# Layer 0's attention in an encoder kernel: the rotary key's products, the conv taps and the modulation pacing are placed anew

## Chip, cores and metric

One core of a Trainium2 chip runs the whole program in one launch. The metric is device time in microseconds (us), the median of several runs; less is better.

## What is computed

Two layers of an encoder on 256 tokens of width 2048, all in float32. Each layer has two halves:

```
mod = silu(c) @ w_mod[l] + b_mod[l]          # six vectors of 2048: shift, scale, gate for each half
h = layer_norm(x) * (1 + scale_m) + shift_m
proj = h @ w_in[l]                            # split into four head groups A, B, C, D
y = concat(gmlp(A), attention(B), short_conv(C), conformer_conv(D)) @ w_out[l]
x = layer_norm(ALPHA * x + (1 + gate_m) * y, post_mix_g, post_mix_b)
h = layer_norm(x) * (1 + scale_f) + shift_f
x = layer_norm(ALPHA * x + (1 + gate_f) * conv_ffn(h), post_ffn_g, post_ffn_b)
```

Group B is latent attention: query and key/value latents are RMS-normed and expanded by `mla_w_uq` and `mla_w_ukv`, a rotary part is added to queries and keys, a masked softmax follows in blocks of 128 queries. Group D's conv has 31 taps along the tokens. `w_mod[l]` alone has 2048 x 12288 numbers, so the six vectors of each layer are a large part of the bytes that the kernel reads.

## The kernel before

Weights are streamed from memory in units of up to 1 MB and multiplied on TensorE (PE) in the order of the program. Layer 0's mixers run through `by_blocks` (L1297) with plain float32 products; most of the rest splits each weight into a high part (`whi`, made on ScalarE, ACT) and a low part (`wlo`, made on VectorE, DVE) and makes three products. Within each engine instructions go in program order; a scheduler fixes that order when the kernel is built. SyncE (SP) issues the loads, also in order.

**Where the attention sits.** After the B group (the latents), the C group (`C_c` products, eight units of 16 products 128 x 256) keeps PE busy while the attention's steps go in between. `mix_b` (L1001) normalises the latents and starts `attend` (L1054), a generator; at each `yield` it puts itself into the list of postponed steps, and one unit of C's products is placed before it goes on. In its first stretch the latents are turned by PE (`ps_q`, `ps_kv`), ACT writes the queries' latents `qg`, DVE writes the rotary key's parts `kc` and the key/value latents `kvr`; PE makes the rotary key `ps_kr` out of `kc`, ACT copies it into `rope`; then follow `ps_qn`, `ps_qr`, `ps_kn`, `ps_v`. A pool of two PSUM buffers serves all of these. Three yields stand between the first two softmaxes and the transposes of their results (`ps_pT`).

**The conv taps.** Group D's 31 taps (`taps`, L859) are queued in a background list and run a few at a time with the units: for a tap ACT makes four activations into a `scaled` buffer (four such buffers) and DVE adds them in one instruction to `convD` (L871). `attended` (L1091) names the instruction behind which ACT's scaled activations are put.

**The modulation stream.** `w_mod`'s blocks of 1 MB are fetched and used in a fixed order: 16 steps for GATE_M (`macc`, L203 and L205), 16 for SHIFT_F, 16 for SCALE_F (L194, each writes a column of sums; the last is followed by the small addition L285 which makes the vector `mod`), then GATE_F, and layer 1's. How many are issued is decided by a credit: `phase` (L311) sets a rate, `pump` (L314) adds it once for each unit loaded and issues one block for each whole credit. `more_mods` (L801) adds the rate `attend` once, and is called four times in `attend`; `mix_b` issues three blocks (MODS_AHEAD) beyond the credit. In layer 0 the units are 8 of B, 8 of C, 8 of `out` (out projection, columns 0 to 1023), 4 of `out_next`, and four of `out_last` with rate 0. What is still missing is forced by `need` (L320), which `out_proj` calls through `before()` after the products of its first token tile: SHIFT_F and SCALE_F must be complete for the norm that follows.

**The end of the out projection.** For each token tile t: `yg`, `x` and the statistics on DVE (L632 to L636), the norm's aggregation (L567), two passes over x (L673, L676), sums of squares on ACT (`junk`, L688), then `xn` (ACT), transposes `ps_xT` (PE, L586), `hN` (scale and shift of the feed-forward's input by `mod`, L118), and the products `first` of the feed-forward (PE, L534).

Of the kernel before, what the change touches and what calls it, by code (L numbers as in the profile page):

```python
# [15 lines left out]
S = 256  # L16
# [16 lines left out]


RATES = [
    dict(B=1.3, attend=1.3, C=1.9, out=1.0, out_next=1.55, out_last=0.0, up=0.7, down=0.7, down_next=0.7, down_last=0.0),
    dict(D=1.0, U=0.0, V=0.0, B=0.0, C=0.0, E=0.9, attend=0.0, out=0.6, out_next=0.6, out_last=0.0, up=0.3, down=0.7, down_next=0.7, down_last=0.0),
]

# [47 lines left out]
def encoder_kernel(ctx: ExitStack, tc: tile.TileContext, A: dict, consts: bass.AP, out: bass.AP):  # L87
# [24 lines left out]
        return accp.tile([P, 512], F32, tag="acc", name=name)  # L112

    def mm(o, lhsT, rhs, start, stop):
        pe.matmul(o, lhsT, rhs, start=start, stop=stop, skip_group_check=True)  # L115

    def ident_act(o, i, scale, bias):
        return act.activation(out=o, in_=i, func=AF.Identity, scale=scale, bias=bias)  # L118
# [1 line left out]
    def slot(name, dtype=F32):  # L120
        return slotp.tile([P, 1024], dtype, tag="slot", name=name)
# [205 lines left out]

    pending = []
    postponed = []
    background = []  # L330

    def flush():
# [79 lines left out]
    def group(w, c0, width, name, then, ntm=0, nk=2, hF=None, bg=0, spare=0):  # L412
# [6 lines left out]
        def products(item, u):  # L419
            if u == 0:  # L420
                box["c"] = [acc_tile(f"{name}_c{i}") for i in range((ncm + 1) // 2)]
                box["t"] = [[acc_tile(f"{name}_t{t}{i}") for i in range(ntm)] for t in range(2)]
                box["h"] = list(hT)
            for part in (range(0, min(4, ncm)), range(4, ncm)):
                for k, (hi, lo) in enumerate(item):
                    kt = u * nk + k
                    st, sp = kt == 0, kt == KT - 1
                    for i in part:
                        o = box["c"][i // 2][:, (i % 2) * S : (i % 2 + 1) * S]
                        off = slice(i * P, (i + 1) * P)  # L430
                        first = st and i % 2 == 0
                        if lo is None:
                            mm(o, hi[:, off], hF(kt), first, sp)
                        else:
                            xh, xl = (h[:, kt % 2, :] for h in box["h"][kt // 2][:2])
                            mm(o, hi[:, off], xh, first, False)
                            mm(o, hi[:, off], xl, False, False)
                            mm(o, lo[:, off], xh, False, sp)
            for k, (hi, lo) in enumerate(item):
                kt = u * nk + k  # L440
                st, sp = kt == 0, kt == KT - 1
                for i in range(ntm):
# [347 lines left out]
    def mixers(l, w_in, Y, hF=None, first_mod=None, quarter=None):  # L790
# [7 lines left out]
        CLB = lambda j: pm[:, 149 + j : 150 + j]  # L798
        attended, stepped = [], []

        def more_mods():  # L801
# [40 lines left out]
        def conv_d(glu):  # L842
# [16 lines left out]
            def taps(k):  # L859
# [7 lines left out]
                for j in range(4):  # L867
                    i = act.activation(out=t[:, j, :n], in_=glu[:, j, :n], func=AF.Copy, scale=CW(k, j))
                    if attended:
                        tc.add_manual_dep(i.ins, attended[0], order_dep, reason="the latents come first")  # L870
                dve.tensor_tensor(out=yd[:, :, 30 - k :], in0=yd[:, :, 30 - k :], in1=t[:, :, :n], op=ALU.add)  # L871

            if hF is not None:
                for k in range(30, -1, -1):
# [126 lines left out]
        def mix_b(wide, narrow):  # L1001
# [14 lines left out]
            if hF is not None:  # L1016
                for _ in range(MODS_AHEAD):
                    next(mods, None)
                stepped.append(last_step[0])

            lat = [tmp_tile("lat0"), tmp_tile("lat1")]
            q01 = tmp_tile("lat2").rearrange("p (t c) -> p t c", t=2)
# [31 lines left out]
        def attend(WQ, WKV, lat, q01, rr):  # L1054
            qg = slot("qg")[:, :768].rearrange("p (j s) -> p j s", j=3)
            kvr = slot("kvr")[:, :768].rearrange("p (j s) -> p j s", j=3)

            def behind(i):
                if stepped:
                    tc.add_manual_dep(i.ins, stepped[0], order_dep, reason="these steps' weights land before the latents turn")  # L1060

            def turn(ps, o, parts):
                for t in range(2):
                    n = parts[t].shape[1]
# [6 lines left out]
                act.activation(out=qg[:, j, :], in_=by, func=AF.Copy, scale=QG(j))  # L1071
            ps = ms_tile("ps_q")
            by = turn(ps, 0, [lat[t][:, 320:448] for t in range(2)])
            act.activation(out=qg[:, 2, :], in_=by, func=AF.Copy, scale=QG(2))
            by = turn(ps, S, [lat[t][:, 256:320] for t in range(2)])
            kc = tmp_tile("kc")
            behind(dve.tensor_tensor(out=kc[0:64, 0:S], in0=by[0:64, :], in1=cosT[0:64, :], op=ALU.mult))
# [4 lines left out]
                behind(dve.tensor_scalar(out=kvr[:, j, :], in0=by, scalar1=KVG(j), scalar2=None, op0=ALU.mult))  # L1082

            rope = slot("rope").rearrange("p (j s) -> p j s", j=4)
            ps = ms_tile("ps_kr")
            mm(ps[:, :S], idup, kc[0:64, 0:S], True, False)
            mm(ps[:, :S], rotdup, kc[0:64, S : 2 * S], False, True)
            pool.memset(rope[64:128, 2, :], 0.0)
            pool.memset(rope[0:64, 3, :], 0.0)
            act.copy(rope[0:64, 2, :], ps[0:64, :S])  # L1090
            attended.append(act.copy(rope[64:128, 3, :], ps[64:128, :S]).ins.name)  # L1091
            more_mods()

            qn = slot("qn").rearrange("p (j s) -> p j s", j=4)
# [99 lines left out]

            p0 = softmax(0, 0)
            p1 = softmax(1, 0)
            yield
            yield
            yield
            turned(p0, 0, 0)  # L1200
# [478 lines left out]
```

## Time and profile before

| | |
|---|---|
| runs | 2221.61, 2224.57, 2225.37 us; median 2224.57 |
| profiled execution | 2224.01 us, of which 2222.2 us are the span in the trace (1.8 us lie around it) |
| mean granted TensorE clock | 0.996 |
| PE busy | 2195.2 us, 99% of the span |
| DVE busy | 1715.7 us, 77% |
| ACT busy | 1092.7 us, 49% |
| bytes moved | 603.96 MB, mean 272 GB/s |

A row of the timeline gives the start, the busy time, engine, line, operation, output and inputs, tile shape and count; in brackets the idle time ahead of it and what ended it. A row of the windows gives a stretch in us, its length, and for each engine the busy time and number of instructions, then the granted TensorE clock (PEclk, 1.00 is full speed), and the share and rate of the DMA engines.

### The profile page before, as it was taken

How to read it: one execution, taken by the hardware profiler on the slowest of the kernel's cores; microseconds unless marked ns; L12 is line 12 of the kernel's file. 1: busy time of each engine (PE TensorE's matmuls, PEld its weight loads, DVE VectorE, ACT ScalarE, POOL GpSimd, SP SyncE). 2: the span in 40 equal slices, each digit the busy share in tenths (PEclk: the TensorE clock that was granted, in tenths of full speed). 3: DMA queues.
4: the chain of work that ended last, by engine and by line, in shares of the span. 5: the costliest groups of instructions: out<-in, count | busy, mean ns of one | idle time of the engine just before them, and what ended most of it. 6: DMA issues, size and time to landing. Idle time of an engine off the chain costs nothing. (4 is left out here: it accounts for less than half of the span.)

```text
span 2222.2 us, 28375 instructions
## 1 busy us (share of the span) xinstructions
PE 2195.2 (99%) x10880; PEld 1803.2 (81%) x10880; DVE 1715.7 (77%) x2197; ACT 1092.7 (49%) x1677; POOL 23.2 (1%) x38
## 2 busy tenths in 40 slices
PE   9999999999999999999999999999999999999997
PEld 6776875588888888888868978868888888888886
DVE  5657996799898989989958988867776656575776
ACT  3132731655554445545655545465455545454552
POOL 0000000000000000000000000000000000000000
PEclk9999999999999999999999999999999999999999
DMA  9999889688988888888758547847765555555553
GB/s 392 417 374 390 336 329 391 222 331 312 339 316 319 327 324 320 316 332 325 281 189 313 175 149 263 323 177 260 262 212 189 180 199 190 190 189 191 191 198 140
DMA packets 94034, 603.96 MB, mean 272 GB/s; under 512 B 10565, under 2 KB 10693, under 8 KB 29125
## 3 DMA queue, kind: packets, MB, share of 16 engines
q1 hardware_dynamic: 93898, 602.15, 73.7%
q8 instruction: 85, 1.39, 0.3%
q14 instruction: 51, 0.42, 0.1%
HBM read 600.01 MB, written 2.10 MB: 271 GB/s over the span
## 5 line engine op out<-in xcount | busy, mean ns | idle before, releaser
L390 ACT CAST whi<-wraw 128x1024 fp32r<-128x1024 f32 (+1 forms) x608 | 634.5, 1047 | 672.9 <-PE g_c L115 202.3
L391 DVE TENSOR_TENSOR wlo<-wraw,whi 128x1024 fp32r<-128x1024 f32 (+1 forms) x608 | 730.4, 1212 | 288.4 <-ACT whi L390 281.6
L115 PE MATMUL v_c<-hT,whi 128*128 128x512 f32 x1408 | 489.6, 391 | 0.0
L115 PE MATMUL g_c<-hT,whi 128*128 128x512 f32 x1280 | 444.7, 391 | 0.0
L115 PE MATMUL v_c<-hT,wlo 128*128 128x256 f32 x1408 | 394.4, 280 | 0.0
L115 PE MATMUL d<-whi,a 128*128 128x512 f32 x1344 | 386.1, 389 | 0.0
L115 PE MATMUL g_c<-hT,wlo 128*128 128x256 f32 x1280 | 358.4, 280 | 0.0
L194 DVE SCALAR_TENSOR_TENSOR wmod<-wmod,crep 128x2048 f32<-128x2048 f32 x128 | 292.0, 2285 | 38.3 <-DMA wmod<-in_w_mod_dram 37.5
L115 PEld LDWEIGHTS v_c<-hT,whi 128*128 128x128 f32 x1408 | 263.3, 187 | 57.6
L115 PEld LDWEIGHTS d<-whi,a 128*128 128x128 f32 x1344 | 252.2, 188 | 52.2
L115 PEld LDWEIGHTS g_c<-hT,whi 128*128 128x128 f32 x1280 | 239.4, 187 | 52.5
L115 PEld LDWEIGHTS v_c<-hT,wlo 128*128 128x128 f32 x1408 | 266.1, 189 | 0.2
L115 PEld LDWEIGHTS g_c<-hT,wlo 128*128 128x128 f32 x1280 | 241.9, 189 | 0.1
L115 PE MATMUL d<-wlo,a 128*128 128x512 f32 x672 | 232.9, 389 | 0.0
L205 DVE SCALAR_TENSOR_TENSOR macc<-wmod,cact,macc 128x2048 f32<-128x2048 f32 x60 | 140.7, 2346 | 19.5 <-DMA wmod<-in_w_mod_dram 19.1
L115 PEld LDWEIGHTS d<-wlo,a 128*128 128x128 f32 x672 | 126.2, 188 | 26.3
L115 PE MATMUL o<-whi,a 128*128 128x512 f32 x320 | 90.5, 390 | 0.0
L410 DVE TENSOR_TENSOR a<-g,a 128x512 fp32r<-128x512 f32 x132 | 88.6, 683 | 0.0
L534 PE MATMUL first<-wexact,hN 128*128 128x512 f32 x192 | 85.5, 595 | 1.2 <-ACT hN L118 0.8
L409 ACT CAST a<-g 128x512 fp32r<-128x512 f32 x132 | 81.1, 615 | 8.3 <-PE d L115 4.8
L1440 DVE SCALAR_TENSOR_TENSOR u<-g,par,u 128x254 f32<-128x254 f32 (+1 forms) x176 | 74.2, 476 | 0.3 <-ACT u L118 0.2
L115 PEld LDWEIGHTS o<-whi,a 128*128 128x128 f32 x320 | 59.9, 188 | 12.7 <-ACT whi L390 0.4
(317 smaller groups left out, 2384.4 us busy)
## 6 DMA issues: line engine op xcount, KB each, us to landing
wmod<-in_w_mod_dram SPq DMA_DIRECT2D x192, 1024.0 KB, 6.8
wraw<-in_ffn_w_up_dram SPq DMA_DIRECT2D x168, 1024.0 KB, 5.4
wraw<-in_ffn_w_down_dram SPq DMA_DIRECT2D x88, 1024.0 KB, 4.9
wexact<-in_w_in_dram SPq DMA_DIRECT2D x64, 512.0 KB, 10.0
wraw<-in_w_in_dram SPq DMA_DIRECT2D x24, 1024.0 KB, 5.2
wraw<-in_w_out_dram SPq DMA_DIRECT2D x22, 1024.0 KB, 5.5
wexact<-in_w_out_dram SPq DMA_DIRECT2D x20, 512.0 KB, 12.4
wexact<-in_ffn_w_up_dram SPq DMA_DIRECT2D x16, 512.0 KB, 6.2
```

The costliest lines, as they stand in the source:

```text
L115: pe.matmul(o, lhsT, rhs, start=start, stop=stop, skip_group_check=True)
L194: i = dve.scalar_tensor_tensor(out=raw, in0=raw, scalar=1.0, in1=crep, op0=ALU.mult, op1=ALU.mult, accum_out=col)
L205: i = dve.scalar_tensor_tensor(out=acc, in0=w, scalar=col, in1=acc, op0=ALU.mult, op1=ALU.add)
L390: held(act.copy(hi[:, :m], r), "cast")
L391: i = dve.tensor_tensor(out=lo[:, :m], in0=r, in1=hi[:, :m].bitcast(F32), op=ALU.subtract)
L409: act.copy(hi, src)
L410: dve.tensor_tensor(out=lo, in0=src, in1=hi.bitcast(F32), op=ALU.subtract)
L534: i = pe.matmul(ps, hN[kt // 4][:, kt % 4, t * P : (t + 1) * P], parts[kt], start=kt == 0, stop=kt == KT - 1, skip_group_check=True,)
L1440: dve.scalar_tensor_tensor(out=u[:, sh:], in0=x[:, : S - sh], scalar=col(k, j), in1=u[:, sh:], op0=ALU.mult, op1=ALU.add)
```

## The change

Five edits, all in layer 0's attention or beside it (line numbers in the rows below: those of the changed kernel are a few higher).

1. The rate of C goes from 1.9 to 2.17, and `mix_b` takes one such rate off the credit.
2. The rotary key's products `ps_kr`, its copies and the first `more_mods` come behind a new `yield`; its first product is ordered behind the last product of a unit of C. (`mm` returns its instruction for that.)
3. One of the three yields behind the first softmaxes goes.
4. The wide tap additions on DVE are ordered behind the third modulation step of `mix_b`, as `kc` and `kvr` are already.
5. `attended` names the activation that writes `qg`'s third part, and no longer the last `rope` copy.

```diff
-    dict(B=1.3, attend=1.3, C=1.9, out=1.0, out_next=1.55, out_last=0.0, ...),
+    dict(B=1.3, attend=1.3, C=2.17, out=1.0, out_next=1.55, out_last=0.0, ...),
...
     def mm(o, lhsT, rhs, start, stop):
-        pe.matmul(o, lhsT, rhs, start=start, stop=stop, skip_group_check=True)
+        return pe.matmul(o, lhsT, rhs, start=start, stop=stop, skip_group_check=True)
...
                         if lo is None:
-                            mm(o, hi[:, off], hF(kt), first, sp)
+                            last_product[0] = mm(o, hi[:, off], hF(kt), first, sp).ins.name
...
-                dve.tensor_tensor(out=yd[:, :, 30 - k :], in0=yd[:, :, 30 - k :], in1=t[:, :, :n], op=ALU.add)
+                behind(dve.tensor_tensor(out=yd[:, :, 30 - k :], in0=yd[:, :, 30 - k :], in1=t[:, :, :n], op=ALU.add))
...
                 for _ in range(MODS_AHEAD):
                     next(mods, None)
                 stepped.append(last_step[0])
+                pace["credit"] -= RATES[l]["C"]
...
-            act.activation(out=qg[:, 2, :], in_=by, func=AF.Copy, scale=QG(2))
+            i = act.activation(out=qg[:, 2, :], in_=by, func=AF.Copy, scale=QG(2))
+            attended.append(i.ins.name)
...
             rope = slot("rope").rearrange("p (j s) -> p j s", j=4)
+            yield
             ps = ms_tile("ps_kr")
-            mm(ps[:, :S], idup, kc[0:64, 0:S], True, False)
+            i = mm(ps[:, :S], idup, kc[0:64, 0:S], True, False)
+            if hF is not None:
+                tc.add_manual_dep(i.ins, last_product[0], order_dep, reason="a unit's products cover the latents' steps")
             mm(ps[:, :S], rotdup, kc[0:64, S : 2 * S], False, True)
...
-            attended.append(act.copy(rope[64:128, 3, :], ps[64:128, :S]).ins.name)
+            act.copy(rope[64:128, 3, :], ps[64:128, :S])
             more_mods()
...
             p0 = softmax(0, 0)
             p1 = softmax(1, 0)
-            yield
             yield
             yield
             turned(p0, 0, 0)
```

How the order moves, at the two places where most of it does. First, PE at the attention's start, before (`ps_kv` are the turned key/value latents, `ps_kr` the rotary key, `C_c` the conv group's accumulators):

```order
L1065 MATMUL ps_kv<-cst,lat_1061 128x128 [waits Activation_49]
L1065 MATMUL ps_kv<-cst,lat_1062 128x128
L115 MATMUL ps_kr<-kc,cst 128x256 [waits DVE_49,PE_49]
L1065 MATMUL ps_kv<-cst,lat_1061 128x128 [waits DVE_49]
L1065 MATMUL ps_kv<-cst,lat_1062 128x128
L115 MATMUL ps_kr<-kc,cst 128x256
L115 MATMUL ps_qn<-qg,wq_1042 128x256 [waits DMAHW4_49,DVE_49]
```

and after the change, at the same place on PE:

```order
L1067 MATMUL ps_kv<-cst,lat_1061 128x128 [waits Activation_49]
L1067 MATMUL ps_kv<-cst,lat_1062 128x128
L115 MATMUL C_c_1094<-hF_115,wexact 128x256 [waits DMAHW4_49]
L115 MATMUL C_c_1094<-hF_115,wexact 128x256
L1067 MATMUL ps_kv<-cst,lat_1061 128x128 [waits DVE_49]
L1067 MATMUL ps_kv<-cst,lat_1062 128x128
L115 MATMUL C_c_1095<-hF_115,wexact 128x256 x2
L115 MATMUL C_c_1094<-hF_115,wexact 128x256 [waits DMAHW5_49]
```

Two products of a C unit stand between the two pairs of `ps_kv`, the other 14 behind them, and the two of `ps_kr` behind those. On ACT, the rotary key's copies (L1096, L1097) stand after the change behind the scaled activations of taps 248 to 240 wide, 33 of them behind the last `qg`; this is the end of that row:

```order
L873 ACTIVATE scaled<-gluD,par 128x241 [waits DVE_49]
L873 ACTIVATE scaled<-gluD,par 128x241 [waits Activation_49] x3
L873 ACTIVATE scaled<-gluD,par 128x240 [waits DVE_49]
L873 ACTIVATE scaled<-gluD,par 128x240 [waits Activation_49]
L1096 COPY rope<-ps_kr 64x256 [waits PE_49]
L1097 COPY rope<-ps_kr 64x256
L873 ACTIVATE scaled<-gluD,par 128x240 [waits Activation_49] x2
```

Before, both copies came directly behind the last `qg`, ahead of all scaled activations.

Second, the end of the out projection. On SP after the change, the loads from the norm's gains (`gb`) on; `wmod_2110` is the last block of SCALE_F:

```order
L643 DMA gb_2064<-in_post_mix_g_dram 128x2048
L643 DMA gb_2066<-in_post_mix_b_dram 128x2048
L375 DMA wexact_2078<-in_ffn_w_up_dram 128x1024
L375 DMA wexact_2080<-in_ffn_w_up_dram 128x1024
L375 DMA wexact_2082<-in_ffn_w_up_dram 128x1024
L375 DMA wexact_2084<-in_ffn_w_up_dram 128x1024
L375 DMA wexact_2086<-in_ffn_w_up_dram 128x1024
L375 DMA wexact_2088<-in_ffn_w_up_dram 128x1024
L375 DMA wexact_2090<-in_ffn_w_up_dram 128x1024
L375 DMA wexact_2092<-in_ffn_w_up_dram 128x1024
L193 DMA wmod_2110<-in_w_mod_dram 128x2048
L295 DMA wmod_2363<-in_w_mod_dram 128x2048
```

Before, that block stood 18 loads of the out projection, gains and feed-forward earlier, right behind the block ahead of it. On DVE before, its step (`wmod_2022`) and the vector's addition (`mod_0_4`) stood here, with the out projection's columns 1024 to 1535:

```order
L636 BN_STATS st_o00_1601<-x0_91 128x6
L632 TENSOR_TENSOR yg_2061<-o0_102410_1969,gate_0_2_1216 128x512
L194 SCALAR_TENSOR_TENSOR wmod_2022,sums_0_4_1597<-wmod_2022,crep_101 128x2048
L633 SCALAR_TENSOR_TENSOR x1_92<-x1_92,yg_2061 128x512
L285 TENSOR_TENSOR mod_0_4_2025<-sums_0_4_1597,par_93 128x16
L636 BN_STATS st_o01_1602<-x1_92 128x6
```

After the change they stand on DVE with the second token tile's last columns, behind the whole norm of the first tile:

```order
L710 SCALAR_TENSOR_TENSOR rs_o0r0_2159<-sums_o00_2141,rs_o0r0_2159 128x1
L633 TENSOR_TENSOR yg_2228<-o0_153610_2047,gate_0_2_1236 128x512
L634 SCALAR_TENSOR_TENSOR x1_92<-x1_92,yg_2228 128x512
L637 BN_STATS st_o01_1602<-x1_92 128x6
L194 SCALAR_TENSOR_TENSOR wmod_2110,sums_0_4_1597<-wmod_2110,crep_101 128x2048
L568 BN_AGGR mv_o0p1_2232<-st_o01_1602 128x2
L285 TENSOR_TENSOR mod_0_4_2113<-sums_0_4_1597,par_93 128x16
```

The step has moved past about twenty instructions of the first tile's norm, and the first tile's `hN` on ACT now names DVE among what it waits for, as it did not before. On PE after the change, `first` is split:

```order
L587 MATMUL ps_xT<-cst,xn 128x128 [waits Activation_49]
L587 MATMUL ps_xT<-cst,xn 128x128 x3
L535 MATMUL first_2211<-wexact,hN_2163 128x512 [waits DMAHW1_49,Activation_49]
L587 MATMUL ps_xT<-cst,xn 128x128 [waits Activation_49]
L587 MATMUL ps_xT<-cst,xn 128x128 x3
L587 MATMUL ps_xT<-cst,xn 128x128 [waits Activation_49]
L587 MATMUL ps_xT<-cst,xn 128x128 x3
L535 MATMUL first_2211<-wexact,hN_2163 128x512
```

Before, four products `first` of `hN_2163` stood ahead of the third and fourth group of `ps_xT`; now one does.

More of the change, by code (lines that the diff above doesn't have):

```diff
@@ L35 @@
 RATES = [
-    dict(B=1.3, attend=1.3, C=1.9, out=1.0, out_next=1.55, out_last=0.0, up=0.7, down=0.7, down_next=0.7, down_last=0.0),
+    dict(B=1.3, attend=1.3, C=2.17, out=1.0, out_next=1.55, out_last=0.0, up=0.7, down=0.7, down_next=0.7, down_last=0.0),
     dict(D=1.0, U=0.0, V=0.0, B=0.0, C=0.0, E=0.9, attend=0.0, out=0.6, out_next=0.6, out_last=0.0, up=0.3, down=0.7, down_next=0.7, down_last=0.0),
@@ L329, in encoder_kernel @@
     postponed = []
+    last_product = [None]
     background = []
@@ L799, in mixers, with behind @@
         attended, stepped = [], []
+        def behind(i):
+            if stepped:
+                tc.add_manual_dep(i.ins, stepped[0], order_dep, reason="these steps' weights land before the latents turn")
         def more_mods():
@@ L1056, in attend @@
             kvr = slot("kvr")[:, :768].rearrange("p (j s) -> p j s", j=3)
-            def behind(i):
-                if stepped:
-                    tc.add_manual_dep(i.ins, stepped[0], order_dep, reason="these steps' weights land before the latents turn")
             def turn(ps, o, parts):
```

## The prediction

> **What bounds the kernel now.** First the page: busy times, then the chain that ended last.
>
> ```profile
> span 2222.2 us, 28375 instructions
> PE 2195.2 (99%) x10880; PEld 1803.2 (81%) x10880; DVE 1715.7 (77%) x2197; ACT 1092.7 (49%) x1677; POOL 23.2 (1%) x38
> ...
> PE 33%; DVE 1%; ACT 0%; issue 0%; DVEq 0%; POOL 0%; ACTq 0%
> ```
>
> PE is busy for all but 2222.2 - 2195.2 = 27.0 us, so a change that removes no product can gain only from idle time and from time at a lowered clock. So I read the timeline of PE where the change works, from 200 us on.
>
> ```profile
> 202.77 0.33 PE L1065 MATMUL ps_q<-cst,lat 128*128 128x128 f32 x1 [0.96 <-ACT lat L1035]
> 202.93 7.07 PE L115 MATMUL C_c<-hF,wexact 128*128 128x256 f32 x32
> ...
> 210.68 0.77 PE L1065 MATMUL ps_q<-cst,lat 128*128 128x128 f32 x4 [0.35 <-ACT qg L1071]
> 211.68 0.44 PE L1065 MATMUL ps_kv<-cst,lat 128*128 128x128 f32 x2 [0.23 <-ACT qg L1071]
> 213.57 1.19 PE L115 MATMUL ps_kr<-kc,cst 64*128 64x256 f32 x2 [1.45 <-DVE kc L1078]
> ...
> 216.52 7.14 PE L115 MATMUL ps_qn<-qg,wq 128*128 128x256 f32 x24
> ```
>
> One unit of C is 16 products, shown as 32 records in 7.07 us: 0.44 us a product. The rotary key waits 1.45 us for `kc`. `ps_qn`, 24 records, takes 7.14 us where 24/32 of 7.07 would be 5.3: a second loss. The windows show it; I cut them where the clock changes, every 3.41 us.
>
> ```profile
> 199.51:202.92 3.41, 2.45 (x9) 1.00 1.04 426
> 209.75:213.16 3.41, 1.79 (x11) 1.00 1.00 414
> 213.16:216.58 3.42, 3.01 (x7) 0.50 1.02 410
> 216.58:219.99 3.41, 3.41 (x8) 0.50 1.02 405
> 219.99:223.40 3.41, 3.41 (x17) 1.00 1.05 430
> 1281.54:1284.95 3.41, 1.44 (x10) 1.00 0.00 0
> 1284.95:1288.36 3.41, 3.23 (x11) 0.50 0.00 0
> 1288.36:1291.78 3.42, 3.42 (x18) 1.00 0.87 307
> ```
>
> The number behind the counts is the granted clock. A window with 1.62 us idle (3.41 - 1.79) was followed by one at 0.50; one with 0.96 idle (3.41 - 2.45) was not. At 0.50, a window with 0.41 idle was followed by a second at 0.50; windows with 0.18 and 0 idle were followed by full speed. I use this as the rule of the case: from between 0.96 and 1.62 us idle the next window runs at half speed, and between 0.18 and 0.41 us of idle within it bring another.
>
> **The attention, what goes.** The 1.45 us wait; and half of the 3.01 + 3.41 = 6.42 us of work done at half speed, 3.2 us. Together 4.7 us, 0.21% of the span: the most that the intended part can give.
>
> **The attention, what comes.** DVE first:
>
> ```profile
> 205.44 7.33 DVE L205 SCALAR_TENSOR_TENSOR macc<-wmod,cact,macc 128x2048 f32<-128x2048 f32 x3 [8.16 <-DMA wmod<-in_w_mod_dram]
> 212.68 0.41 DVE L1077 TENSOR_TENSOR kc<-ps_q,cst 64x256 f32<-64x256 f32 x1
> ...
> 213.34 0.47 DVE L1082 TENSOR_SCALAR kvr<-ps_kv,par 128x256 f32<-128x256 f32 x1
> ```
>
> `kc` and the first `kvr` stand behind three modulation steps, and stay there. The first `kvr` ends at 213.81. In the changed order, the second pair of `ps_kv` waits for it, with only two products of C ahead: 211.9 + 0.9 = 212.8, so 1.0 us idle, about 0.4 of it ahead of 213.16. That window then has 0.35 + 0.23 + 0.4 = 1.0 us idle, near the 0.96 that cost nothing: I take no drop. Then 14 products (6.2 us) end near 220.2, `ps_kr` near 221.1, the first half of `ps_qn` near 223.7. The tap additions, now behind the third step, stand behind that first `kvr` too and delay none of this. Now ACT:
>
> ```profile
> 216.56 0.36 ACT L1090 COPY rope<-ps_kr 64x256 f32<-64x256 f32 x1 [4.93 <-PE ps_kr L115]
> ...
> 217.33 2.85 ACT L868 ACTIVATE scaled<-gluD,par 128x248 f32<-128x248 f32 x7
> ...
> 224.41 7.49 ACT L868 ACTIVATE scaled<-gluD,par 128x245 f32<-128x245 f32 x19
> ```
>
> A scaled activation takes 2.85/7 = 0.41 to 7.49/19 = 0.39 us. With `attended` moved, 33 of them stand ahead of the two `rope` copies: from the last `qg`, near 211.6, 33 x 0.40 = 13.1 us, so the copies run from 224.7 to 225.5. The second half of `ps_qn` needs the PSUM buffer that they read, from 223.7: PE waits 1.8 us, all of it inside the window 223.40 to 226.82. That is above 1.62, so I take one window at half speed, a loss of 1.7. Sum: -4.7 + 1.0 + 1.8 + 1.7 = **-0.2**. Ends: -1.9 without the drop, +1.5 with a second half-speed window.
>
> The yield that goes brings the transposes `ps_pT` one unit (7.07 us) nearer to the softmax. Bounds: nothing, or the rest of the chain of DVE and ACT; two units, 14.1 us, still cover it, and I take nothing.
>
> By the Trainium skill (TensorE: Matmul & The Clock Gate, Part 1: The HAM clock gate) the clock halves only after an idle window of about 3.4 us, and the window runs freely. The rows above differ on the first: 1.62 us idle in a window was enough here. By the page's rule the attention's 1.8 us wait would cost no clock, and the attention would give -1.9. On the second they agree: all the cuts fit one grid of 3.41 us.
>
> **The pacing.** Before, layer 0's credit up to the last units: 8 x 1.3 + 8 x 1.9 + 4 x 1.3 + 8 x 1.0 + 4 x 1.55 = 45.0, and 45 + 3 blocks ahead = 48 = 16 each of GATE_M, SHIFT_F and SCALE_F: just enough. After: 8 x 2.17 - 2.17 = 15.19 takes the place of 15.2, the sum is 44.99, and 47 blocks are paced. The last block of SCALE_F is left for `need`, behind eight loads of `w_out`, two of `gb` and eight of `ffn_w_up`.
>
> The two rows are SP's timeline, which issues the loads:
>
> ```profile
> 374.83 18.63 SPq L374 DMA_DIRECT2D wexact<-in_ffn_w_up_dram  x8
> 393.56 1.22 SPq L295 DMA_DIRECT2D wmod<-in_w_mod_dram  x2
> ```
>
> The second view is the windows, with PE, PEld, DVE, ACT and POOL ahead of the clock:
>
> ```profile
> 404.00:405.00 1.00, 1.00 (x4) 0.50 (x3) 0.93 (x2) 1.00 (x4) 0.00 (x0) 1.00 0.30 123
> ```
>
> In that place two other blocks were issued from 393.56 and the DMA engines fall quiet in the window from 404 (share 0.30, 123 GB/s); the first of the two must have landed near 402. Its step is then placed on DVE:
>
> ```profile
> 375.86 2.28 DVE L194 SCALAR_TENSOR_TENSOR wmod<-wmod,crep 128x2048 f32<-128x2048 f32 x1
> ...
> 403.97 0.69 DVE L636 BATCH_NORM_STATS2 st_o<-x 128x6 f32<-128x512 f32 x1
> 404.70 0.26 DVE L567 BATCH_NORM_AGGREGATE mv_o0p<-st_o 128x2 f32<-128x24 f32 x1
> ```
>
> Before, the step ran from 375.86, 27 us ahead of its use. After, the step stands between the two rows at 404: from 404.6, 2.28 us, the aggregation, then the addition: `mod` near 407.3. Who waits for it:
>
> ```profile
> 402.45 2.90 ACT L118 ACTIVATE hN<-ps_xT,mod,mod 128x128 f32<-128x128 f32 x8 [0.95 <-PE ps_xT L586]
> ```
>
> `hN` started at 402.45; now not before 407.35, and its eight run to 410.3. On PE:
>
> ```profile
> 401.81 1.04 PE L586 MATMUL ps_xT<-cst,xn 128*128 128x128 f32 x8
> 402.96 3.70 PE L534 MATMUL first<-wexact,hN 128*128 128x512 f32 x8
> 406.50 1.04 PE L586 MATMUL ps_xT<-cst,xn 128*128 128x128 f32 x8
> 407.38 10.46 PE L534 MATMUL first<-wexact,hN 128*128 128x512 f32 x24
> 417.68 1.04 PE L586 MATMUL ps_xT<-cst,xn 128*128 128x128 f32 x8
> ```
>
> PE stands from 402.85 to 407.8 (5.0 us against 0.1), makes one `first` (0.43 us), and the fourth group of `ps_xT` needs the PSUM buffer that the second four `hN` read until 410.3. From about 410.4 there remain four transposes (0.45) and 31 `first` at 10.30/24 = 0.43 (13.3 us): the second tile's `ps_xT` start at 424.1 and not 417.68: **+6.4**. The second tile's norm is 2.3 us later on DVE and does not become the bound, since PE is 6.4 later. This idle fills the window 404.31 to 407.72 (the same grid) wholly, so the clock falls at 407.72. Within that half-speed window PE still idles about 0.7 us between `first` and the two groups of transposes, more than 0.41, so by the case's rule the next one is slow too: 0.4 for the first (its other work is waiting anyway) and 1.7 for the second. **+8.5** in all; bounds +6.4 and +8.5.
>
> **Behind it.** The late block also takes one of four `raw` buffers:
>
> ```profile
> 426.31 1.28 DVE L203 TENSOR_SCALAR macc<-wmod,cact 128x2048 f32<-128x2048 f32 x1
> ```
>
> The second `wraw` of the next stage is issued when this step has given its buffer back; after the change one more step (2.4 us, the row of three: 7.33/3) must run first. Bounds 0 and 2; the steps' blocks now have 6 us more to land and run, so I take 0. The remaining program keeps its order but for a shift of one step, and I take nothing for it.
>
> **Sum.** Against the profiled execution: 2224.0 - 0.2 + 8.5 = **2232.3**. That execution lies 0.56 below the median of the runs, 2224.57.
>
> **Rivals.** A measurement of this kernel can tell about 0.2%, 4.4 us: 2220.1 to 2229.0 count as no change.
> - *The change works as meant* and the late block is hidden: 2224.0 - 4.7 = 2219.3, faster. It needs `mod` ready by 402.45, that is its step done on DVE ahead of the second tile's `yg` and not behind it; the order speaks against it, and so does the load, which lands near 402. Chance 0.05.
> - *The attention pays in full*, because ACT runs the scaled activations later or `ps_qn` does not wait for the copies, and the late block costs as above: 2224.0 - 4.7 + 8.5 = 2227.8, no change. ACT is in order and the 33 stand first, which speaks against. Chance 0.15.
> - *The clock holds* in the attention and falls for one window only at the late block: 2224.0 - 1.9 + 6.4 + 0.4 = 2228.9, on the edge of no change. For it: in layer 1, 1.97 us idle cost one window, not two. Chance 0.2, split evenly between no change and slower. By the Trainium skill's rule on the clock (the page named above) it would come out so, since only the wait near 408 fills a whole window.
> - *Everything drops*: a second slow window in the attention and the full 2 us for `wraw`: 2224.0 + 1.5 + 8.5 + 2 = 2236.0. Chance 0.1.
>
> My forecast has the remaining 0.5 (2229.5 to 2234). Faster 0.05; no change 0.15 + 0.10 = 0.25; slower 0.70. The range reaches from just below the second rival to just below the last, 2226.5 to 2235.5.
>
> **What would show it.** Right: on PE an idle row of some 5 us ahead of `first` near 408, released by ACT `hN`; on DVE the L194 step behind the last statistics; in the attention no wait for `kc`, a wait of about 1 us at the second `ps_kv` and one near 1.8 us inside `ps_qn`, released by ACT; a clock of 0.50 behind the wait at 408. Wrong: `hN` near 402 with no wait for DVE; a full clock throughout; or a new wait of PE in the stage behind 425 us.

## The result, and the profile after

| | before | after |
|---|---|---|
| runs on one chip, median of 5 | 2223.16 us (2221.61 to 2225.37) | 2232.47 us (2229.25 to 2234.63) |
| profiled execution | 2224.01 us, span 2222.2 | 2233.07 us, span 2230.9 |
| mean granted TensorE clock | 0.996 | 0.996 |

The ratio is 1.0037, with a 95% interval of 1.0027 to 1.0048: slower by 6 to 10.7 us, as forecast (2232.3). How much of that agreement is luck is what the rest is about. First the page of after, busy times by engine:

```profile
span 2230.9 us, 28359 instructions
PE 2197.3 (98%) x10880; PEld 1801.5 (81%) x10880; DVE 1715.6 (77%) x2197; ACT 1092.8 (49%) x1677; POOL 25.4 (1%) x38
```

The span is 8.7 us longer; PE's busy time grew by 2.1 and its idle time from 27.0 to 33.6. To place the 8.7 us I compare when PE reaches the same instruction in both traces. The attention's start lies 0.5 us earlier in after already (its first `C_c` at 202.41 against 202.93), ahead of the first edit, so 0.5 is taken off each difference below.

**The attention.** PE's timeline of after; the bracket is the idle time ahead of the row and what ended it:

```profile
213.04 0.44 PE L1067 MATMUL ps_kv<-cst,lat 128*128 128x128 f32 x2 [0.47 <-DVE kvr L1085]
213.31 6.21 PE L115 MATMUL C_c<-hF,wexact 128*128 128x256 f32 x28
...
220.51 2.86 PE L115 MATMUL ps_qn<-qg,wq 128*128 128x256 f32 x12
224.72 2.86 PE L115 MATMUL ps_qn<-qg,wq 128*128 128x256 f32 x12 [1.36 <-ACT rope L1097]
```

ACT's timeline of after, the scaled activations and the last copy that the second `ps_qn` waits for:

```profile
211.10 12.94 ACT L873 ACTIVATE scaled<-gluD,par 128x248 f32<-128x248 f32 x33
...
224.31 0.37 ACT L1097 COPY rope<-ps_kr 64x256 f32<-64x256 f32 x1
```

The windows of after at that wait, PE alone: length, busy time and count, granted clock, share and rate of the DMA engines:

```profile
221.64:225.06 3.42, 2.06 (x11) 1.00 0.98 404
225.06:228.47 3.41, 3.21 (x15) 1.00 0.34 67
```

Both foretold waits are there, behind `kvr` (0.47) and behind the 33 activations and the copies (1.36), but the clock stayed at full speed: each half of `ps_qn` takes 2.86 us, where all 24 records took 7.14 in before, with half clock up to 219.99. The next mark is `ps_mean`, behind C's last product: 292.72 against 295.50, so the attention and C gain 2.78 - 0.52 = **2.26 us**.

**Given back.** The out projection follows. PE's timeline of before:

```profile
295.50 1.89 PE L115 MATMUL ps_mean<-convD,ones 128*128 128x256 f32 x8
...
313.47 0.73 PE L115 MATMUL o<-wlo,a 128*128 128x512 f32 x2
...
319.50 0.59 PE L115 MATMUL ps_rD<-dgD,ones 128*128 128x256 f32 x2
```

and of after:

```profile
292.72 1.89 PE L115 MATMUL ps_mean<-convD,ones 128*128 128x256 f32 x8
294.92 14.00 PE L115 MATMUL o<-wexact,ya 128*128 128x512 f32 x32 [0.31 <-DMA wexact<-in_w_out_dram]
...
312.64 0.73 PE L115 MATMUL o<-wlo,a 128*128 128x512 f32 x2 [1.47 <-DVE wlo L392]
...
318.69 0.59 PE L115 MATMUL ps_rD<-dgD,ones 128*128 128x256 f32 x2
```

At `ps_rD` the lead is down from 2.78 to 0.81 us: **1.97 given back**, 0.31 to a load of `w_out` and 1.47 to the first low part `wlo`, which DVE makes. DVE's timeline of before between C's end and that `wlo`, the first and the last of four steps (two more of the kind start at 299.46 and 305.58):

```profile
296.38 2.28 DVE L194 SCALAR_TENSOR_TENSOR wmod<-wmod,crep 128x2048 f32<-128x2048 f32 x1
...
309.98 2.29 DVE L194 SCALAR_TENSOR_TENSOR wmod<-wmod,crep 128x2048 f32<-128x2048 f32 x1
...
312.19 2.36 DVE L391 TENSOR_TENSOR wlo<-wraw,whi 128x1024 fp32r<-128x1024 f32 x2
```

The same stretch of after (two more steps start at 299.02 and 305.41):

```profile
292.74 2.28 DVE L194 SCALAR_TENSOR_TENSOR wmod<-wmod,crep 128x2048 f32<-128x2048 f32 x1
...
295.94 2.29 DVE L194 SCALAR_TENSOR_TENSOR wmod<-wmod,crep 128x2048 f32<-128x2048 f32 x1
...
309.15 2.29 DVE L194 SCALAR_TENSOR_TENSOR wmod<-wmod,crep 128x2048 f32<-128x2048 f32 x1
...
311.36 2.36 DVE L392 TENSOR_TENSOR wlo<-wraw,whi 128x1024 fp32r<-128x1024 f32 x2
```

Behind C's last product DVE has five steps ahead of `wlo` where it had four: C ends 2.78 us earlier, `wlo` only 0.83. In all, both traces have 19 such steps (L194) between 238 us and `wlo`; the fifth is the one that before ran from 292.88, while PE was still at C's last products.

**The late block.** The end of the out projection in after, first PE's timeline:

```profile
400.99 1.04 PE L587 MATMUL ps_xT<-cst,xn 128*128 128x128 f32 x8
406.84 2.07 PE L535 MATMUL first<-wexact,hN 128*128 128x512 f32 x2 [4.82 <-ACT hN L118]
...
424.47 1.04 PE L587 MATMUL ps_xT<-cst,xn 128*128 128x128 f32 x8
```

DVE's, with the late step:

```profile
403.14 0.69 DVE L637 BATCH_NORM_STATS2 st_o<-x 128x6 f32<-128x512 f32 x1
403.76 2.27 DVE L194 SCALAR_TENSOR_TENSOR wmod<-wmod,crep 128x2048 f32<-128x2048 f32 x1
...
406.13 0.12 DVE L285 TENSOR_TENSOR mod<-sums,par 128x16 f32<-128x16 f32 x1
```

and ACT's:

```profile
406.33 2.91 ACT L118 ACTIVATE hN<-ps_xT,mod,mod 128x128 f32<-128x128 f32 x8 [5.08 <-issue]
```

The step stands where the prediction put it, behind the last statistics and with no gap, so not waiting for its load. `mod` is there at 406.25, ACT starts `hN` 0.08 us later (its bracket names no releaser, but `mod` is what it lacked), and PE has stood for 4.82 us. The windows of after, PE alone:

```profile
402.55:405.96 3.41, 0.00 (x0) 1.00 0.16 65
405.96:409.37 3.41, 2.53 (x6) 0.50 0.65 228
409.37:412.78 3.41, 3.41 (x9) 0.50 0.55 180
```

Two windows at half clock (the next is at full speed); half of the work in them is (2.53 + 3.41) / 2 = 3.0 us lost. From one group of `ps_xT` to the other (400.99 to 424.47) it is 23.48 us, before 417.68 - 401.81 = 15.87: **7.6 us more**. Behind it the trace of after loses 1.9 us more up to its end. So: -0.5 - 2.3 + 2.0 + 7.6 + 1.9 = 8.7.

### The profile page after: what moved, and what is told of

Same layout as the page of the kernel before. It is cut to its first block, busy times and chain, and to the rows that moved or that the text cites. A ratio compares the mean times of both kernels' runs of the same rounds, so it can differ in the third digit from the quotient of the medians.

```text
span 2230.9 us, 28359 instructions
## 1 busy us (share of the span) xinstructions
PE 2197.3 (98%) x10880; PEld 1801.5 (81%) x10880; DVE 1715.6 (77%) x2197; ACT 1092.8 (49%) x1677; POOL 25.4 (1%) x38
## 3 DMA queue, kind: packets, MB, share of 16 engines
q8 instruction: 85, 1.39, 0.2%
## 5 line engine op out<-in xcount | busy, mean ns | idle before, releaser
L194 DVE SCALAR_TENSOR_TENSOR wmod<-wmod,crep 128x2048 f32<-128x2048 f32 x128 | 292.2, 2285 | 43.3 <-DMA wmod<-in_w_mod_dram 41.0
L535 PEld LDWEIGHTS first<-wexact,hN 128*128 128x128 f32 x192 | 36.0, 194 | 46.9 <-issue 35.2
```

The source lines that it names most:

```text
L194: i = dve.scalar_tensor_tensor(out=raw, in0=raw, scalar=1.0, in1=crep, op0=ALU.mult, op1=ALU.mult, accum_out=col)
L535: i = pe.matmul(ps, hN[kt // 4][:, kt % 4, t * P : (t + 1) * P], parts[kt], start=kt == 0, stop=kt == KT - 1, skip_group_check=True,)
```

## The experiments

**The theory** after this reading: the whole loss is the late block, and what the attention gains is lost again at the first `wlo` to DVE's work. **Rivals**: the attention itself pays nothing, or the five edits cost something elsewhere. Every ratio is against the kernel before on the same chip, with its 95% interval; a median is of 11 runs where nothing else is said.

**e1_48_blocks**: the changed kernel, with the rate of C set so that the credit reaches 48 blocks, and nothing else.

```diff
-    dict(B=1.3, attend=1.3, C=2.17, ...),
+    dict(B=1.3, attend=1.3, C=2.1715, ...),
```

> The changed kernel with the rate of C at 2.1715 instead of 2.17, so that the credit makes 45.0 and the last SCALE_F block is paced like before. Theory (the late block costs some 7.6 us at the norm and 2 to 3 us more in the feed-forward behind it, while the attention's gain of about 2.3 us is mostly given back at the out projection's first split weights): 2222 to 2224 us, no idle row ahead of the first products near 403. Rival (the rest of the change is what costs, the pacing only moves the wait elsewhere): 2229 us or more. Second rival (the attention's gain is kept whole once the block is in time): 2220.5 us.

Measured: 2224.88 us against 2224.96, 0.9996 [0.9987, 1.0004]. A change of 0.0015 in a rate takes the whole loss away. It gains nothing that can be told over before though: PE still waits in the out projection, and here a half-clock window follows. PE's timeline of e1:

```profile
295.85 14.00 PE L115 MATMUL o<-wexact,ya 128*128 128x512 f32 x32 [0.80 <-DMA wexact<-in_w_out_dram]
309.68 1.84 PE L115 MATMUL ps_var<-ones,sqD 128*128 128x1 f32 x16
...
313.07 0.93 PE L115 MATMUL o<-wlo,a 128*128 128x512 f32 x2 [0.97 <-DVE wlo L392]
```

and its windows, PE alone:

```profile
310.03:313.44 3.41, 2.44 (x18) 1.00 0.87 296
313.44:316.86 3.42, 3.42 (x10) 0.50 0.95 388
```

0.80 + 0.97 + 1.7 of half clock is 3.5, more than the attention's 2.3.

**e2_late_block_alone**: the kernel before, with only its credit brought to 44.99.

```diff
-    dict(B=1.3, attend=1.3, C=1.9, ...),
+    dict(B=1.3, attend=1.3, C=1.89875, ...),
```

> The kernel before with only the rate of C changed from 1.9 to 1.89875: the credit is 44.99 and the last SCALE_F block is forced late; the attention is as before, with its wait for the rotary key and its two slow windows. Theory: 2223.2 + 7.6 + 2 to 3 = 2232.5 to 2234 us, with the wait of some 5 us ahead of first and two windows at half clock behind it. Rival (the late block costs little by itself and the new attention's order costs the rest): below 2228 us.

Measured: 2230.32 us, 1.0029 [1.0020, 1.0038], 5.4 us slower with none of the other edits. The same wait is there, to the hundredth (PE's timeline):

```profile
407.57 2.08 PE L534 MATMUL first<-wexact,hN 128*128 128x512 f32 x2 [4.82 <-ACT hN L118]
```

It falls differently on the grid: the wait ends at 407.57, where a window begins; that one is at half clock with PE busy throughout (3.41), the next at full speed. One slow window, not two, so 4.8 + 1.7 = 6.5 at the place by the rows. The median lies between the two expectations (2232.5 to 2234, or below 2228): the 2 to 3 us that the theory added for the feed-forward did not come, and one slow window is missing.

**e3_rope_copies_first**: e1, with `attended` on the last `rope` copy again, as before the change.

```diff
-            i = act.activation(out=qg[:, 2, :], in_=by, func=AF.Copy, scale=QG(2))
-            attended.append(i.ins.name)
+            act.activation(out=qg[:, 2, :], in_=by, func=AF.Copy, scale=QG(2))
...
-            act.copy(rope[64:128, 3, :], ps[64:128, :S])
+            attended.append(act.copy(rope[64:128, 3, :], ps[64:128, :S]).ins.name)
```

> As e1, with attended again the last rope copy, so ACT makes the rotary key's copies ahead of the scaled taps. Theory that the gain is given back at the out projection whatever the attention saves: the wait of 1.4 us inside ps_qn goes, the total stays within 0.7 us of e1, and the wait for wlo near 310 grows or the taps end later. Rival (each us saved in the attention is a us off the total): 1.4 us below e1.

Measured: 2228.57 us, 1.0015 [1.0007, 1.0024]; 3.6 us slower. The wait inside `ps_qn` went (24 records in 5.45 us without a gap), but at the end of C another came:

```profile
297.36 2.08 PE L115 MATMUL ps_mean<-convD,ones 128*128 128x256 f32 x4 [6.18 <-DVE convD L876]
```

Neither expectation had such a loss; the theory had named later taps, but within 0.7 us of e1. PE makes `ps_kr` at 220.04 in that run, so ACT does not start the scaled activations until 222 where they started at 211.10, and the chain of 31 taps (ACT, then an addition on DVE) ends 6.2 us too late for the conv's mean. So edit 5 belongs to edit 2: the 1.36 us wait is the price of taps that end in time.

**e4_fewer_steps_ahead**: e1, with fewer modulation steps issued in C and more in the out projection.

```diff
-    dict(B=1.3, attend=1.3, C=2.1715, out=1.0, out_next=1.55, ...),
+    dict(B=1.3, attend=1.3, C=1.6, out=1.5001, out_next=1.55, ...),
```

> As e1, with fewer modulation steps paced in C and more in the out projection (C 1.6, out 1.5001; the sum stays 45): three steps of 2.28 us less stand on DVE ahead of the first wlo of the out projection. Theory (DVE's row of modulation steps is what holds wlo, and so what takes the attention's gain back): the wait for wlo near 310 goes and the total is 1.5 to 2 us below e1, if the steps that come later do not meet another wait. Rival (the wait comes from the loads of w_out or from ACT): same as e1 within 0.5 us, with the wait still there.

Measured: 2227.81 us, 1.0016 [1.0008, 1.0025]. The wait at the first `wlo` went, and three came behind it: 1.39 at 318.55 and 1.54 at 332.35 for `wlo`, and this one for ACT, with a half-clock window behind it:

```profile
345.37 0.74 PE L115 MATMUL o<-whi,a 128*128 128x512 f32 x2 [2.73 <-ACT whi L391]
```

The steps do not vanish; put beside the splits of other weights they hit those.

**e5_changed_again**: the changed kernel unaltered, beside other runs and with a profile of its own (median of 7).

> The changed kernel unaltered, a second profile and a second set of times on the chip that also runs e6 to e8. Theory: about 7 us above the kernel before, and again a wait of 4.8 us ahead of first near 407. What is open is the rest: in its first profile PE's pairs of products (512 and 256 columns) took 0.353 us instead of 0.347 from 440 to 550 us, about 2 us in all. If that belongs to the change's order of buffers it shows again; if it belongs to the single execution it may be gone.

Measured: 2231.93 us against 2225.05, 1.0029 [1.0018, 1.0040], 6.9 us slower. The 4.82 us wait is there again (`first` at 409.47), with two half-clock windows behind it; and two more slow windows at the first `wlo`, where the first profile of this kernel had none. Its windows there, PE alone:

```profile
308.77:312.18 3.41, 3.07 (x20) 1.00 0.84 300
312.18:315.59 3.41, 2.46 (x6) 0.50 0.73 269
315.59:319.00 3.41, 3.41 (x10) 0.50 1.04 396
```

It also bears on the 1.9 us behind the late block. The costliest group of the feed-forward's first products between 440 and 550 us (records, busy us and mean ns of one) is this in before:

```profile
L115 PE MATMUL v_c<-hT,whi 128*128 128x512 f32 x177 | 61.5, 391 | 0.0
```

in the profile of after:

```profile
L115 PE MATMUL v_c<-hT,whi 128*128 128x512 f32 x178 | 62.5, 398 | 0.0
```

in that of e5:

```profile
L115 PE MATMUL v_c<-hT,whi 128*128 128x512 f32 x176 | 60.9, 392 | 0.0
```

and in that of e1:

```profile
L115 PE MATMUL v_c<-hT,whi 128*128 128x512 f32 x178 | 62.7, 397 | 0.0
```

The same products took 1.8% longer in after, 7 ns a record; over the 306 high-part records of the stretch (`v_c` and `g_c`) that is 2.1 us. The profiled executions of e1 (397) and e3 (396) show it too; the others have 391 to 394. e5 is the same program as after and does not show it, so the program alone does not bring it.

**e6_one_step_fewer**: e1, with one step less ahead of the first `wlo` and the credit made up in `out`.

```diff
-    dict(B=1.3, attend=1.3, C=2.1715, out=1.0, ...),
+    dict(B=1.3, attend=1.3, C=1.9, out=1.2376, ...),
```

> As e1 (credit 45.0), with C 1.9 and out 1.2376: one modulation step less stands on DVE ahead of the out projection's first wlo, where e4 had three less. Theory (DVE is full from the attention to about 350 us, and its steps must be placed where PE does not wait for them): the wait near 313 shrinks or goes, the later waits of e4 stay away or are under 1 us, total 1 to 2.5 us below e1. Rival (any step that is put later meets another wait): e1 or slower, with waits for wlo or whi between 318 and 350.

Measured: 2226.85 us, 1.0009 [1.0000, 1.0018]. The scheduler now puts the conv's `ps_rD` ahead of the first weights, and PE waits for it and then for `wlo` all the same:

```profile
312.06 0.70 PE L115 MATMUL ps_rD<-dgD,ones 128*128 128x256 f32 x2 [1.62 <-DVE dgD L929]
...
314.81 0.73 PE L115 MATMUL o<-wlo,a 128*128 128x512 f32 x2 [1.12 <-DVE wlo L392]
```

**e7_bias_on_pool**: e1, with one addition of a bias row (1 x 2048) moved from DVE to GpSimd.

```diff
-                dve.tensor_tensor(out=acc[0:1, :], in0=acc[0:1, :], in1=row[0:1, :], op=ALU.add)
+                (pool if (l, m) == (0, GATE_M) else dve).tensor_tensor(
+                    out=acc[0:1, :], in0=acc[0:1, :], in1=row[0:1, :], op=ALU.add
+                )
```

> As e1, with the addition of the gate's bias row (one row of 2048, 2.27 us on DVE in the attention, L301) done by GpSimd. Theory (DVE's row of work sets when wlo comes): 2.3 us of DVE work less ahead of the out projection, so the wait for wlo near 313 goes, and with it any slow window behind it: 1 to 3 us below e1, 2 to 3 below the kernel before. Rival (the wait comes from the loads): as e1.

Measured: 2228.41 us, 1.0015 [1.0007, 1.0024]. It was meant to free DVE and did the opposite. GpSimd's timeline of e7 at that place:

```profile
236.09 4.49 POOL L301 TENSOR_TENSOR macc<-macc,brow 1x2048 f32<-1x2048 f32 x1 [30.48 <-DVE macc L205]
```

and DVE's, an ordinary tap addition and the one beside it:

```profile
232.28 1.14 DVE L878 TENSOR_TENSOR convD<-convD,scaled 128x952 f32<-128x952 f32 x1
...
236.27 5.33 DVE L878 TENSOR_TENSOR convD<-convD,scaled 128x948 f32<-128x948 f32 x1
```

The addition on DVE starts 0.18 us behind GpSimd's and takes 5.33 us instead of 1.14; it ends at 241.60, which is GpSimd's end (240.58) and 1.02 more. PE then waits 3.15 us for DVE's `rope`, with a half-clock window after it, and the wait for `wlo` (1.35 at 317.93) is still there.

**e8_two_taps_out**: e1, without the last two taps (median of 10).

```diff
-                    background.append(lambda k=k: taps(k))
+                    background.append((lambda: None) if k in (0, 1) else (lambda k=k: taps(k)))
```

> As e1, with the last two of the 31 conv taps left out (their two additions on DVE, 1.1 us each, and eight scaled activations on ACT): a part of group D's convolution is not computed. Theory (DVE): the wait for wlo near 313 goes, as in e7, total 1 to 3 us below e1. Rival (loads): as e1, the wait stays.

Measured: 2224.76 us, 0.9999 [0.9990, 1.0008]. The wait for the first `wlo` stays (1.25), and DVE is only idle longer ahead of it (1.55 us in e1):

```profile
286.24 0.69 DVE L411 TENSOR_TENSOR a<-yb,a 128x512 fp32r<-128x512 f32 x1 [3.57 <-ACT a L410]
```

This was against the theory as I had put it, that any work taken from DVE ahead of `wlo` would do. DVE stands idle for 3.57 us at 286 and for 0.44 at C's end; so by this reading only what stands **between C's last product and `wlo`** counts. The theory was narrowed to that, and the next kernel tries it.

**e9_two_steps_cheap**: e1, with two of the steps in that stretch cut to 128 of their 2048 columns.

```diff
+        n = 128 if (l, m, kt) in ((0, SCALE_F, 0), (0, SCALE_F, 1)) else D
...
-            out=raw, in0=raw, scalar=1.0, in1=crep, op0=ALU.mult, op1=ALU.mult, accum_out=col
+            out=raw[:, :n], in0=raw[:, :n], scalar=1.0, in1=crep[:, :n], op0=ALU.mult, op1=ALU.mult, accum_out=col
```

> As e1, with the first two SCALE_F steps working on 128 of their 2048 columns (two values of the scale come out wrong): the loads, their order and all else stay, but 4.3 us of DVE work go from the stretch between the end of the C group (292) and the first wlo (311). e8 showed that DVE work saved ahead of 285 only makes DVE wait for PE. Theory (between PE's end of C and the first wlo stand five modulation steps where before there were four, and this chain of DVE is what takes the attention's gain back): no wait for wlo near 313 and no slow window behind it, 1 to 3 us below e1. Rival (loads or ACT): the wait stays, same as e1.

Measured: 2221.09 us against 2225.45, 0.9982 [0.9973, 0.9991], 4.4 us faster. Such a step now takes 0.29 us. DVE stands idle for 1.40 us ahead of `wlo`, until ACT has made `whi`, so it is no longer what holds PE, and the first low product follows without a gap (PE):

```profile
312.10 0.63 PE L115 MATMUL o<-wlo,a 128*128 128x512 f32 x2
```

No wait, and no slow window. The profiled execution, 2221.75 us, is 2.3 below that of before, the attention's gain; why the medians lie 4.4 apart was not traced. This names the place; it is no version to use, since part of the sums is left out.

**e10_step_to_out_next** and **e11_two_to_out_next**: e1, with one or two steps moved out of that stretch into `out_next`.

```diff
-    dict(B=1.3, attend=1.3, C=2.1715, out=1.0, out_next=1.55, ...),
+    dict(B=1.3, attend=1.3, C=2.03, out=1.0, out_next=1.7976, ...),     # e10
+    dict(B=1.3, attend=1.3, C=1.9, out=1.0, out_next=2.0251, ...),      # e11
```

> As e1, with C 2.03 and out_next 1.7976 (the sum stays 45.0): four modulation steps, not five, between the C group's end and the first wlo, and the missing one in the out projection's second part, where DVE idles for 5 to 9 us at a time. Theory as for e9: the wait near 313 is under 0.3 us, no new wait as in e4 and e6 since those put the step into the first part; 1 to 3 us below e1 and the kernel before. Rival (every step that is put later meets a wait): as e6, 2 us above e1.

> As e10 with C 1.9 and out_next 2.0251: three steps between the C group's end and the first wlo. Theory: no wait near 313; the same as e10 within 0.7 us, since one step less already takes the wait away. Rival: the later blocks now come too late for the vector at the norm, with a wait of several us ahead of first near 403.

Measured: e10 2225.91 us, 1.0002 [0.9993, 1.0011]; e11 2229.81 us, 1.0025 [1.0016, 1.0034]. In both the wait for `wlo` is gone and the one for `ps_rD` of e6 is there again (e10, PE; a half-clock window follows):

```profile
312.19 1.22 PE L115 MATMUL ps_rD<-dgD,ones 128*128 128x256 f32 x2 [1.61 <-DVE dgD L929]
```

In e11 three blocks of `w_mod`, one more than in e10, stand on SP ahead of the last eight loads of `w_out`, and PE waits for those too, again with a half-clock window behind. The wait ahead of `first` that the rival named did not come.

```profile
377.72 5.37 PE L115 MATMUL o<-wexact,ya 128*128 128x512 f32 x8 [2.77 <-DMA wexact<-in_w_out_dram]
```

**e12_step_late_order_kept**: e10, with three orders added that keep `ps_rD` and its neighbours on DVE where they were, behind the first weights.

```diff
+                    tc.add_manual_dep(i.ins, splits[1], order_dep, ...)     # rd, behind the first pair of wlo
...
-                mm(box["r"][:, :S], ones, box["dg"][:, :S], True, True)
+                i = mm(box["r"][:, :S], ones, box["dg"][:, :S], True, True)
+                if hF is not None:
+                    tc.add_manual_dep(i.ins, sums_done[7], order_dep, ...)  # behind the first unit's products
...
+                        tc.add_manual_dep(i.ins, splits[3], order_dep, ...) # convD by r, behind the second pair
```

> As e10 (C 2.03, out_next 1.7976: one modulation step goes from ahead of the first wlo to the out projection's second part), with the variance's small steps (rd, ps_rD and the products with it) held by order dependencies where e1 and the kernel before have them, behind the first weights' low parts; e10 had let them move ahead and PE waited 1.6 us for dgD. Theory (the chain of DVE between the C group's end and the first wlo takes the attention's gain back, as e9 showed): no wait of over 0.3 us between 300 and 330 and no slow window there; 2 to 3.5 us below the kernel before (2222 to 2223.5 if that is at 2225.4). Rival (the step that is put off meets another wait): at the kernel before's time or above it.

Measured: 2222.43 us against 2224.66, 0.9992 [0.9983, 1.0001]. The first low product on PE:

```profile
311.24 0.62 PE L115 MATMUL o<-wlo,a 128*128 128x512 f32 x2
```

No wait there, and none between 229 and 372 us; the next is 0.49 us at 372.74, for a load of `w_out`. The 2.2 us are about what the attention gained. It is the best whole version of the study, clearly faster than the changed kernel; against the kernel before the interval just reaches 1, so that "faster than before" is likely and not shown.

## Why the prediction was right, and where it was not

| term | predicted | measured (profiled execution of after) |
|---|---|---|
| wait for `kc`, half clock of before | -4.7 | gone |
| wait for `kvr` | +1.0 | 0.47 |
| wait of `ps_qn` for the copies | +1.8 | 1.36 |
| slow window behind it | +1.7 | 0 |
| attention | -0.2 | -2.3 |
| late block | +8.5 | +7.6 |
| second `wraw` | 0 | 0.2 idle |
| rest of the program | 0 | +2.0 in the out projection, some 1.9 behind the late block, most of it slower products |

- **The late block**: the credit of 44.99, the place of the step on DVE, and the wait of about 5.0 us came as worked out (4.82). e1 takes the block back and the loss is gone; e2 makes the block late alone and is 5.4 us slower. The cause is shown. The size was 0.9 too high: the second wait that I had put behind it, some 1.5 us for the fourth group of `ps_xT`, did not come, since no gap stands there: at half clock the work ahead of that group lasted until its buffer was free. The lowered clock took 3.0 us and not 0.4 + 1.7. The second slow window came, but not for the reason given, idle time between `first` and the transposes: the 0.88 us idle in the first one (405.96 to 409.37) is the end of the 4.82 us wait itself. The grid of windows lies elsewhere in each execution (an edge at 404.31 in before, 402.55 in after, 404.16 in e2), and in e2 the wait ended on an edge and one window was slow. So whether one or two fall is where the grid happens to lie, and the two of the forecast are in part luck.
- **The attention**: both waits were found on the right engines, both shorter. The step that failed is "above 1.62, so I take one window at half speed": the wait was 1.36 us, between the 0.96 that had cost nothing and the 1.62 that had cost a window, and no window fell; this much of the rival *The clock holds* came true. Nor is idle time a sure measure: 1.79 us idle in a window of e6 (from 310.63) and 1.86 in one of e7 (from 1287.87) cost no clock either, 1.55 in one of e2 (from 1291.62) did. So the part paid 2.3 and not 0.2, past the end of -1.9 that the prediction gave for it.
- **"The remaining program keeps its order but for a shift of one step, and I take nothing for it"** failed too, in the other direction; no term stood for the stretch between C and the norm. Behind the attention PE arrived 2.3 us earlier, but DVE's chain of steps did not: one step more of it now stood behind C's last product, and PE waited. e9 shows the mechanism by shrinking those steps, e8 that two additions less ahead of that stretch do not help, and e12 that the gain stays if the step moves and the order is kept. The +2.0 here and the attention's -2.3 come to -0.3, where I had -0.2.
- **The yield** and the second **`wraw`** cost about nothing, as taken: there is no wait ahead of `ps_pT`, and 0.2 us for the weights although that issue comes at 437.28, 9.7 us later.
- **The clock at the late block**: an idle window (in e5 idle for 3.1 of its 3.41 us) gave one slow window where PE then was busy in all of it (e2, 3.41), and two where it still idled (0.88 us in after, 1.72 in e5). That is the rule used, though its bound by idle time does not hold everywhere: in e8 a slow window with 0.44 us idle (from 312.47) was the only one, where 0.41 in before brought a second. By the Trainium skill (TensorE: Matmul & The Clock Gate, Part 1: The HAM clock gate) an idle window of some 3.4 us halves the clock; the wait here fits that, but e5's first `wlo` does not: 0.34 us idle in its window, and the next ran at 0.50.

The mechanism of the large term is shown, but that 2232.3 lies so near to the median is luck. Against the forecast the attention is off by -2.1 us, the out projection by +2.0, the late block by -0.9, the stretch behind it by +1.9 and the start by -0.5, which comes to +0.4.

The median of the first set is 9.3 us above before, that of e5 6.9, and their intervals overlap; by the rows, without the slower products, the change costs some 7 us.

## What to carry to other kernels

A credit that only just reaches its count (45.0) is a threshold: a rate that is off by 0.0015 puts a whole block behind everything that `need` forces, so do that sum whenever a rate is touched. A gain on the busiest engine is worth only what is left at the next place where another engine's chain joins it: follow it there and count what that chain does between the last thing that it waits for and the join. When such a step is moved, look where the scheduler puts its neighbours; here four of five ways to move it (e4, e6, e10, e11) made a new wait of over 1 us, and one that also pinned the order (e12) did not.

## What the hardware showed that I had not expected

**The clock falls with little idle time when the products are tiny.** 0.97 us idle (e1) and 0.34 (e5) in a window were followed by half clock; 1.36 and 1.47 in after were not (windows from 221.64 and from 310.39, the latter with 1.94 busy). What sets e1 and e5 apart is that their windows hold most or all of `ps_var`, 16 records of one column that fill 1.84 us of the timeline. In after those lie in the window from 306.98, with no idle time, and it cost nothing. The other profiles bear it out. Six windows at full clock hold seven or more of these records and 0.34 to 1.62 us idle, and the next ran at half clock (e1, e5, e7, e8, e10, e11); a seventh, with 12 of them and 0.34 idle (e10, from 1376.84), did not bring it. Without any of them, no window of the 14 profiles with less than 1.55 us idle was followed by half clock. So these products seem to count as less than busy; the rows bracket this and don't give the rule, and no kernel was made that changes `ps_var` alone.

**GpSimd can stop DVE.** In e7 DVE's addition from two SBUF tensors ended one ordinary duration behind GpSimd's, as if it began only then. The Trainium skill (SBUF — State Buffer, SBUF: two separate sides) says that such an instruction and one of GpSimd that reads SBUF take turns on a shared port, each for its whole length; 5.33 us beside 4.49 and 1.14 agrees. On GpSimd the one-row addition took 4.49 us.

**Some executions run their products 1.8% slower for 100 us**, 396 to 398 ns against 391 (after, e1 and e3, from 440 to 550 us), at a full granted clock of 1.00. That is 2 us, as large as the gains in question, and its cause stayed open.
